# Sparse attention of a decoder trunk: probabilities times values in plain fp32 on two halves of TensorE's columns, in place of split fp32r products

## The chip, the core and the metric

The kernel runs on one core of one Trainium2 chip, as one launch. Its time is the device time of that core in microseconds (us). The program is built with a scheduling layer: the code says what each instruction does, and a scheduler decides within the dependences in which order the instructions of one engine stand. The engines run side by side, each through its own queue in order; semaphores that the layer inserts make one wait for another.

## The reference, cut to what matters

Two layers over 1024 tokens of width 1024, in float32. The second is native sparse attention: 16 heads of 64 in two groups that share keys and values. Every group of heads has three attentions over its keys, a compressed one (63 key blocks), a selected one (eight blocks of 64 keys) and a window of 512 keys, and their outputs are added with gates:

```python
o_cmp, p_cmp = compressed_attention(q, k_cmp, v_cmp, slopes)
o_slc = selected_attention(q, ks, vs, p_cmp, slopes)
o_win, _ = banded_attention(q, kw, vw, slopes, WIN_SIZE - 1, 1)
...
o = gates[..., 0:1] * o_cmp + gates[..., 1:2] * o_slc + gates[..., 2:3] * o_win
o = o.transpose(0, 3, 1, 2, 4).reshape(b, s, NSA_WIDTH).astype(x.dtype)
ym = memory_attention(qm, rms_norm(mem, mem_norm_g), w_mem_kv)
y = jnp.concatenate([o * jax.nn.silu(z), ym * jax.nn.silu(zm)], axis=-1)
return x + (y.astype(x.dtype) @ w_out)
```

The change is in the product of the probabilities with the values, for all three attentions, and in what prepares its two operands.

## The kernel before, in words

The first two thirds of the time are layer one and the projections of layer two (`proj`, L228, with `proj_step`, L238). Matmuls there and elsewhere are made from fp32r operands in split form: a value is rounded into a high part and the rest is a low part, and three products (high by high, high by low, low by high) stand for one of full precision.

`nsa_vals` (L1266) projects the values of both selected and window attention, 128 tokens at a time, and splits them: `vraw` is scaled by ScalarE, GpSimd rounds it into the first 64 columns of a `nv` tile (L1292, through L226) and puts the rest into the other 64 (L1293). So the weights of a later product hold 64 columns of high parts and 64 of low parts. `compress_v` (L1375) makes the same of the compressed values (`vc`).

`nsa_attention` (L1617) goes through 128 works. A work is one block of 128 queries of one group (`it`, 16 of them), one quad of heads, one branch (window or selected) and one pair of heads. A work has 1 to 8 blocks of 128 keys (`key_range`, L1483): 528 block-works in all. Its steps:

- `nsa_scores` (L1489): scores of two heads on TensorE (L1515); VectorE adds the mask and takes the minimum (L1524); ScalarE takes the exponential (L1526); VectorE the reciprocal of the sum (L1529); GpSimd scales by it and by the gate (L1532). Works are scored up to three ahead.
- `nsa_apply` (L1535): for two key blocks at a time TensorE transposes the probabilities of both heads into a PSUM bank `t` (L1545), ScalarE copies the bank to `ph` with rounding (L1549), VectorE subtracts `ph` from the bank into `pl` (L1550). The batch goes into a list `pend`, and the batch four places back (`DELAY = 3`) is multiplied.
- `nsa_av` (L1557): the product. For each key block one matmul with `ph` and one with `pl`, 256 columns (two heads) by weights of 128 columns, into an accumulator `acc`; the compressed part opens it (L1566). After the last key block of a quad ScalarE copies and VectorE adds the halves into `ot` (L1577, L1578), which joins high and low parts, and GpSimd multiplies it into the gate path `y` (L1581).

```python
        o = self.o[:, 256 * pair:256 * pair + 256]
        for x in (ph, pl):
            for i, k in enumerate(kbs):
                nc.tensor.matmul(o, V[:, k0 + k, :], x[:, 256 * i:256 * i + 256], start=False,
                                 stop=(br == 1 and k == nb - 1 and x is pl), skip_group_check=True)
```

Next to that, `nsa_cmp` (L1400) computes the compressed attention of a query block two ahead: its probabilities `ce` are transposed in eight pieces of 64 columns (L1449), copied and split into `pc` (L1450, L1451). As filler for TensorE, the loop runs projections of the second half of the tokens (`fill_proj`, L1781) and later the output projection of the first half (`out_half`, L1091, through `out_step` L1134). `out_tail` (L1141) is the output projection of the second half, which ends the program. The order in the code is the order of these calls; the scheduler moves instructions within what buffers (two or three `t` banks, two `acc` banks, nine `h` tiles for `ph`, `pl` and others) and data allow.

Of the kernel before, what the change touches and what calls it, by code (L numbers as in the profile page):

```python
# [38 lines left out]
BACK = 2  # L39
PAUSE = (1, 3, 5, 0)  # L40
LOOK = (3, 3, 2, 3)
DELAY = 3
FILL0, FILL1 = (4, 3, 2.2, 1.8), (3.2,)
CMPW = 2

# [1 line left out]
def f32(ap):  # L47
    return ap.bitcast(F32)


class Trunk:
# [1024 lines left out]
    def split_pair(self, half, p):  # L1076

        if (half, p) not in self.ys:
            for b in self.pend:
                h, g, _ = self.its[b[0][0]]  # L1080
                assert (h, 2 * g + b[0][1]) != (half, p)
            y = self.Y[half][p]
            self.Y[half][p] = None
            h = self.u("yh", F32R, (128, 2, 512))
            l = self.u("yl", F32R, (128, 2, 512))
            self.nc.scalar.activation(h, y, AF.Copy)  # L1086
            self.nc.vector.tensor_tensor(l, y, f32(h), op=ALU.subtract)
            self.ys[half, p] = (h, l)
        return self.ys[half, p]
# [176 lines left out]
    def nsa_vals(self, x, rcol):  # L1266
        nc = self.nc
        ws = []
        for i, kn in enumerate((3, 3, 2)):
            h, l = self.w()  # L1270
            ws += [(h[:, j, :], l[:, j, :]) for j in range(kn)]
        V = [[self.u("nv", F32R, (128, 8, 128)) for _ in range(2)] for _ in range(2)]
        self.gates = self.const.tile([128, 8, 48], F32, name="gates")
        half = self.small([128, 8], "half", bufs=1)
        nc.vector.tensor_scalar(half, rcol, 0.5, None, op0=ALU.mult)
        for tb in range(8):
            ps = self.big()
            for k in range(8):
                xh, xl = x[k][tb // 4]
                wh, wl = ws[k]  # L1280
                for i, (xx, w) in enumerate(((xh, wh), (xl, wh), (xh, wl))):
                    nc.tensor.matmul(ps[:, :304], xx[:, tb % 4 * 128:tb % 4 * 128 + 128], w,
                                     start=(k == 0 and i == 0), stop=(k == 7 and i == 2))
                if k % 4 == 3:
                    self.tick()
            nc.scalar.activation(self.gates[:, tb, :], ps[:, 256:304], AF.Tanh, scale=half[:, tb:tb + 1])
            v = self.h("vraw", F32, (128, 256))
            nc.scalar.activation(v, ps[:, :256], AF.Copy, scale=rcol[:, tb:tb + 1])
            for b in range(2):
                for g in range(2):  # L1290
                    o = 128 * b + 64 * g
                    self.round_to(V[b][g][:, tb, 0:64], v[:, o:o + 64])  # L1292
                    nc.gpsimd.tensor_tensor(V[b][g][:, tb, 64:128], v[:, o:o + 64],  # L1293
                                            f32(V[b][g][:, tb, 0:64]), op=ALU.subtract)
        self.V = V
        nc.vector.tensor_scalar(self.gates, self.gates, 0.5, 0.5, op0=ALU.mult, op1=ALU.add)

# [77 lines left out]
    def compress_v(self, ops):  # L1375
# [14 lines left out]
        for g in range(2):  # L1390
            p = self.bank()
            for c in range(2):
                nc.tensor.matmul(p[:, :64], h[:, c, g, :], w2[:, c, :], start=(c == 0), stop=(c == 1))
            v = self.const.tile([128, 128], F32R, name=self.n("vc"))
            nc.scalar.activation(v[:, 0:64], p[:, :64], AF.Copy)
            nc.vector.tensor_tensor(v[:, 64:128], p[:, :64], f32(v[:, 0:64]), op=ALU.subtract)
            out.append(v)
        self.vcmp = out

    def nsa_cmp(self, it):  # L1400
# [41 lines left out]
            nc.gpsimd.tensor_tensor(e, e, mx[:, 3, :, None].to_broadcast([128, 8, 64]), op=ALU.mult)  # L1442
        for _ in range(1 + CMPW):
            yield
        pcs = self.u("pc", F32R, (128, 2, 512))
        for quad in range(2):
            t = self.bank()
            for h in range(4):
                nc.tensor.transpose(t[:64, 128 * h:128 * h + 128], e[:, 4 * quad + h, :], self.ident)  # L1449
            nc.scalar.activation(pcs[0:64, quad], t[:64], AF.Copy)  # L1450
            nc.vector.tensor_tensor(pcs[64:128, quad], t[:64], f32(pcs[0:64, quad]), op=ALU.subtract)  # L1451
            yield
        self.pc[it] = pcs

    def nsa_query(self, it):
# [79 lines left out]
    def nsa_apply(self, W):  # L1535

        nc = self.nc
        nb = self.key_range(W)[1]
        for kb in range(0, nb, 2):
            kbs = list(range(kb, min(kb + 2, nb)))  # L1540
            w = 256 * len(kbs)
            t = self.bank()
            for i, k in enumerate(kbs):
                for h in range(2):
                    nc.tensor.transpose(t[:, 256 * i + 128 * h:256 * i + 128 * h + 128],  # L1545
                                        W["e"][h][:, 128 * k:128 * k + 128], self.ident)
            ph = self.h("ph", F32R)
            pl = self.h("pl", F32R)
            nc.scalar.activation(ph[:, :w], t[:, :w], AF.Copy)  # L1549
            nc.vector.tensor_tensor(pl[:, :w], t[:, :w], f32(ph[:, :w]), op=ALU.subtract)  # L1550
            self.pend.append((W["key"], kbs, nb, ph, pl))
            if len(self.pend) > DELAY:
                self.nsa_av(self.pend.pop(0))
            yield
        W["e"] = None

    def nsa_av(self, batch):  # L1557
        nc = self.nc
        key, kbs, nb, ph, pl = batch
        it, quad, br, pair = key  # L1560
        half, g, qb = self.its[it]
        k0 = self.key_range({"key": key})[0]
        V = self.V[1 - br][g]
        if br == 0 and pair == 0 and kbs[0] == 0:
            self.o = self.acc()
            nc.tensor.matmul(self.o, self.vcmp[g], self.pc[it][:, quad], start=True, stop=False,  # L1566
                             skip_group_check=True)
        o = self.o[:, 256 * pair:256 * pair + 256]
        for x in (ph, pl):
            for i, k in enumerate(kbs):  # L1570
                nc.tensor.matmul(o, V[:, k0 + k, :], x[:, 256 * i:256 * i + 256], start=False,  # L1571
                                 stop=(br == 1 and k == nb - 1 and x is pl), skip_group_check=True)
        if br == 1 and pair == 1 and kbs[-1] == nb - 1:
            av = self.o.rearrange("p (c e q) -> p c e q", c=2, e=2)
            tmp = self.h("ot", F32, (128, 2, 128))
            for e in range(2):
                nc.scalar.activation(tmp[64 * e:64 * e + 64], av[64 - 64 * e:128 - 64 * e, :, e, :], AF.Copy)  # L1577
                nc.vector.tensor_tensor(tmp[64 * e:64 * e + 64], av[64 * e:64 * e + 64, :, e, :],  # L1578
                                        tmp[64 * e:64 * e + 64], op=ALU.add)
            y = self.Y[half][2 * g + quad][:, :, qb % 4 * 128:qb % 4 * 128 + 128]  # L1580
            nc.gpsimd.tensor_tensor(y, y, tmp, op=ALU.mult)  # L1581

    def seg_load(self, seg):

# [32 lines left out]
    def nsa_attention(self, fill0, fill1):  # L1617
# [38 lines left out]
        for i, W in enumerate(works):  # L1656
# [27 lines left out]
            for sc in new:  # L1684
                run(sc)
            run(ap)
            if i % 8 == 7:
                self.AB.pop(it)
        while self.pend:
            self.nsa_av(self.pend.pop(0))  # L1690
        run(fill)

    def layer2_plan(self):
# [284 lines left out]
```

## Time and profile before

| what | us |
|---|---|
| median of 3 runs (1974.09 to 1976.76) | 1975.76 |
| the profiled execution, its own time | 1974.66 |
| its span, first to last instruction | 1972.9 |
| TensorE, busy share of the span | 96% |
| VectorE / ScalarE / GpSimd, busy share | 60% / 43% / 42% |
| attention stage, 1265 to 1905 us | 640 |

A profile's matmul row begins when the matmul starts to stream and ends when its last result has landed; matmuls overlap in the pipeline, so the mean duration of one is longer than the time from one start to the next. The latter, called pace here, is what a row of a dense sequence divided by its count gives. "PEld" is the loading of weights, which runs beside the matmuls. A line names the line of the kernel, the engine, the operation, and output <- inputs.

### The profile page before, as it was taken

The page shows a single profiled execution, that of the slowest core. Times are in us where ns is not written, and L with a number is a line of the kernel's source. Part 1 is how long each engine was busy: PE and PEld are TensorE (multiplying, and loading weights), DVE is VectorE, ACT ScalarE, POOL GpSimd, SP SyncE. Part 2 cuts the span into 40 slices and gives each one's busy share as a digit, 9 for nine tenths or more (in the row PEclk, how much of TensorE's full clock was granted, in tenths as well). Part 3 has the DMA queues.
Part 4 walks back from the last instruction along what each step waited for, and adds up shares of the span by engine and source line. Part 5 has one row for each costly group of instructions (what it writes and reads, how often), then busy time and mean ns, then how long its engine had stood idle before and what let it go on. Part 6 is the DMA issues. An engine that isn't in the chain of part 4 may idle for free. (4 is left out here: it accounts for less than half of the span.)

```text
span 1972.9 us, 27378 instructions
## 1 busy us (share of the span) xinstructions
PE 1885.7 (96%) x10018; PEld 1592.9 (81%) x10018; DVE 1187.7 (60%) x2293; ACT 840.0 (43%) x1780; POOL 824.7 (42%) x941
## 2 busy tenths in 40 slices
PE   8999999999999999999999999999988999989997
PEld 6789988887877777888888878787777787877886
DVE  7544336535344856561153574678688877889864
ACT  4210024423213623330044351467558666788851
POOL 6241102223124434322224433576676555567533
PEclk9999999999999999999999999999999999999998
DMA  4123310113110111132223413222231112210013
GB/s 177 61 97 122 114 53 33 33 54 107 54 51 25 43 43 43 42 131 81 78 74 93 138 60 112 75 75 70 65 94 57 49 49 80 89 57 33 12 58 99
DMA packets 57286, 141.90 MB, mean 72 GB/s; under 512 B 8256, under 2 KB 16960, under 8 KB 57152
## 3 DMA queue, kind: packets, MB, share of 16 engines
q1 hardware_dynamic: 57152, 140.16, 22.0%
q8 instruction: 79, 1.29, 0.3%
q14 instruction: 55, 0.45, 0.1%
HBM read 120.21 MB, written 19.92 MB: 71 GB/s over the span
## 5 line engine op out<-in xcount | busy, mean ns | idle before, releaser
L220 POOL TENSOR_SCALAR wh<-raw 128x1024 fp32r<-128x1024 f32 (+2 forms) x149 | 170.2, 1144 | 644.6 <-PE big L244 272.0
L221 DVE TENSOR_TENSOR wl<-raw,wh 128x1024 fp32r<-128x1024 f32 (+4 forms) x151 | 193.9, 1287 | 173.2 <-POOL wh L220 150.7
L1532 POOL TENSOR_SCALAR P<-P,nden,gates 128x640 f32<-128x640 f32 (+7 forms) x256 | 211.4, 835 | 136.3 <-DVE nden L1529 115.9
L244 PE MATMUL big<-xh,wh 128*128 128x512 f32 x752 | 259.0, 424 | 2.0 <-ACT xh L301 1.5
L244 PE MATMUL big<-xl,wh 128*128 128x512 f32 x752 | 243.4, 399 | 1.0 <-DVE xl L302 1.0
L244 PE MATMUL big<-xh,wl 128*128 128x512 f32 x752 | 234.4, 393 | 0.0
L1526 ACT ACTIVATE P<-P,nden 128x640 f32<-128x640 f32 (+7 forms) x256 | 187.6, 733 | 89.8 <-DVE nden L1524 84.4
L1550 DVE TENSOR_TENSOR pl<-t,ph 128x512 fp32r<-128x512 f32 (+1 forms) x304 | 183.7, 615 | 36.6 <-ACT ph L1549 32.6
L1549 ACT ACTIVATE ph<-t 128x512 fp32r<-128x512 f32 (+1 forms) x304 | 159.3, 533 | 58.9 <-PE t L1545 48.8
L1545 PE MATMUL t<-ident,P 128*128 128x128 f32 x1056 | 167.3, 277 | 16.5 <-DVE pl L1550 13.7
L244 PEld LDWEIGHTS big<-xl,wh 128*128 128x128 f32 x752 | 141.7, 189 | 32.4 <-DVE xl L302 2.6
L1545 PEld LDWEIGHTS t<-ident,P 128*128 128x128 f32 x1056 | 125.7, 141 | 50.5 <-DVE pl L1550 12.8
L244 PEld LDWEIGHTS big<-xh,wl 128*128 128x128 f32 x752 | 141.8, 189 | 30.1 <-DVE wl L221 0.2
L244 PEld LDWEIGHTS big<-xh,wh 128*128 128x128 f32 x752 | 135.3, 190 | 37.3 <-issue 14.9
L244 PE MATMUL big<-x,wh 128*128 128x512 f32 x480 | 144.3, 395 | 0.0
L1571 PE MATMUL acc<-ph,nv 128*128 128x256 f32 x528 | 129.1, 312 | 6.2 <-ACT ph L1549 5.9
L1571 PE MATMUL acc<-pl,nv 128*128 128x256 f32 x528 | 122.6, 300 | 0.0
L1524 DVE CUSTOM_DVE_ANT_0 P<-big,mask 128x640 f32<-128x640 f32 (+3 forms) x128 | 116.8, 914 | 3.6 <-PE big L1515 2.2
L244 PEld LDWEIGHTS big<-x,wh 128*128 128x128 f32 x480 | 87.8, 188 | 16.4
L1571 PEld LDWEIGHTS acc<-ph,nv 128*128 128x128 f32 x528 | 87.1, 192 | 13.8 <-ACT ph L1549 11.4
L524 DVE SCALAR_TENSOR_TENSOR df<-big,row 128x1024 f32<-128x1024 f32 x23 | 39.9, 1737 | 93.2 <-PE big L244 88.6
L244 PE MATMUL f<-x,wh 128*128 128x512 f32 x288 | 94.1, 405 | 0.0
(341 smaller groups left out, 4199.9 us busy)
## 6 DMA issues: line engine op xcount, KB each, us to landing
raw<-nw_f SPq DMA_DIRECT2D x42, 512.0 KB, 3.5
raw<-hw_dv SPq DMA_DIRECT2D x24, 512.0 KB, 3.5
raw<-hw_dil SPq DMA_DIRECT2D x22, 512.0 KB, 3.6
raw<-now SPq DMA_DIRECT2D x32, 256.0 KB, 2.7
raw<-hw_z SPq DMA_DIRECT2D x14, 512.0 KB, 3.4
raw<-how SPq DMA_DIRECT2D x16, 448.0 KB, 3.4
raw<-hw_xa SPq DMA_DIRECT2D x8, 512.0 KB, 3.5
res<-xT SPq DMA_DIRECT2D x8, 512.0 KB, 5.1
```

Source lines behind the costliest of these rows:

```text
L220: e.tensor_scalar(h[:, k0:k1], raw[:, k0:k1], 1.0, 0.0, op0=ALU.mult, op1=ALU.add)
L221: nc.vector.tensor_tensor(l[:, k0:k1], raw[:, k0:k1], f32(h[:, k0:k1]), op=ALU.subtract)
L244: self.nc.tensor.matmul(o, w[:, k, :], v, start=(k == 0 and i == 0), stop=(k == 7 and i == 2))
L524: self.nc.vector.scalar_tensor_tensor(ot[:, sl], p.rearrange("p (i r) -> p i r", r=dil), sc, rt[:, sl], op0=ALU.mult, op1=ALU.mult)
L1524: nc.vector.tensor_tensor_reduce(ev, sv, mv, scale=1.0, scalar=3e38, op0=ALU.add, op1=ALU.min, accum_out=den[:, 0, h:h + 1])
L1526: nc.scalar.activation(e, e, AF.Exp, bias=den[:, 0, h:h + 1], scale=-1.0, accum_out=den[:, 1, h:h + 1])
L1532: nc.gpsimd.tensor_scalar(es[h], es[h], den[:, 2, h:h + 1], gt[:, 2 - br, hh:hh + 1], op0=ALU.mult, op1=ALU.mult)
L1545: nc.tensor.transpose(t[:, 256 * i + 128 * h:256 * i + 128 * h + 128], W["e"][h][:, 128 * k:128 * k + 128], self.ident)
L1549: nc.scalar.activation(ph[:, :w], t[:, :w], AF.Copy)
L1550: nc.vector.tensor_tensor(pl[:, :w], t[:, :w], f32(ph[:, :w]), op=ALU.subtract)
L1571: nc.tensor.matmul(o, V[:, k0 + k, :], x[:, 256 * i:256 * i + 256], start=False, stop=(br == 1 and k == nb - 1 and x is pl), skip_group_ch ...
```

## The change

What is no longer made: the split of the values (`vraw`, L1292, L1293), of the compressed values, of the probabilities (`pl`) and of the compressed probabilities. `nv` becomes two plain fp32 tiles. The transposed probabilities are copied once, into `pt`: by VectorE for the second pair of key blocks of a work (`kb == 2`), by ScalarE for the others. The product is a plain fp32 matmul for each key block and each head: 64 columns of weights, 128 columns of moving data, head 0 into partitions 0 to 63 of the accumulator (the first half of TensorE's columns) and head 1 into partitions 64 to 127 (the second half). The compressed part has one block-diagonal weight tile for the two heads. VectorE multiplies the accumulator into `y` straight from PSUM. The products of a work are issued together, after the next work's transposes, once at least four key blocks are waiting (`BURST`, `nsa_due`); nothing ties them to each other beyond that.

```diff
-DELAY = 3
+BURST = 4
@@ nsa_vals
-            v = self.h("vraw", F32, (128, 256))
-            nc.scalar.activation(v, ps[:, :256], AF.Copy, scale=rcol[:, tb:tb + 1])
-            for b in range(2):
-                for g in range(2):
-                    o = 128 * b + 64 * g
-                    self.round_to(V[b][g][:, tb, 0:64], v[:, o:o + 64])
-                    nc.gpsimd.tensor_tensor(V[b][g][:, tb, 64:128], v[:, o:o + 64],
-                                            f32(V[b][g][:, tb, 0:64]), op=ALU.subtract)
+            nc.scalar.activation(V[tb // 4][:, tb % 4], ps[:, :256], AF.Copy, scale=rcol[:, tb:tb + 1])
@@ compress_v
+            v = self.const.tile([128, 128], F32, name=self.n("vc"))
+            nc.gpsimd.memset(v, 0.0)
+            for e in range(2):
+                nc.scalar.activation(v[64 * e:64 * e + 64, 64 * e:64 * e + 64], p[64 * e:64 * e + 64, :64], AF.Copy)
@@ nsa_cmp
+        t = self.bank()
+        for c in range(4):
+            nc.tensor.transpose(t[:, 128 * c:128 * c + 128], e[:, 2 * c:2 * c + 2, :].rearrange("p h n -> p (h n)"),
+                                self.ident)
+        pcs = self.u("pc", F32, (128, 512))
+        nc.scalar.activation(pcs, t, AF.Copy)
@@ nsa_apply
-            nc.scalar.activation(ph[:, :w], t[:, :w], AF.Copy)
-            nc.vector.tensor_tensor(pl[:, :w], t[:, :w], f32(ph[:, :w]), op=ALU.subtract)
-            self.pend.append((W["key"], kbs, nb, ph, pl))
-            if len(self.pend) > DELAY:
-                self.nsa_av(self.pend.pop(0))
+            pt = self.h("pt")
+            if kb == 2:
+                nc.vector.tensor_copy(pt[:, :w], t[:, :w])
+            else:
+                nc.scalar.activation(pt[:, :w], t[:, :w], AF.Copy)
+            W["p"] += [pt[:, 256 * i:256 * i + 256] for i in range(len(kbs))]
+            yield
+        W["e"] = None
+        self.pend.append(W)
+
+    def nsa_due(self, W=None):
+
+        due = [w for w in self.pend if w is not W]
+        if due and (W is None or sum(len(w["p"]) for w in due) >= BURST):
+            quad = due[0]["key"][:2]
+            while self.pend and self.pend[0] is not W and self.pend[0]["key"][:2] == quad:
                 self.nsa_av(self.pend.pop(0))
@@ nsa_av
+        c = 128 * (1 - br) + 64 * g
+        for k, pt in enumerate(W["p"]):
+            v = self.V[(k0 + k) // 4][:, (k0 + k) % 4, c:c + 64]
+            for h in range(2):
+                nc.tensor.matmul(self.o[64 * h:64 * h + 64, 128 * pair:128 * pair + 128], v,
+                                 pt[:, 128 * h:128 * h + 128], start=False,
+                                 stop=(br == 1 and k == nb - 1), skip_group_check=True)
-                nc.scalar.activation(tmp[64 * e:64 * e + 64], av[64 - 64 * e:128 - 64 * e, :, e, :], AF.Copy)
-                nc.vector.tensor_tensor(tmp[64 * e:64 * e + 64], av[64 * e:64 * e + 64, :, e, :],
-                                        tmp[64 * e:64 * e + 64], op=ALU.add)
-            nc.gpsimd.tensor_tensor(y, y, tmp, op=ALU.mult)
+            nc.vector.tensor_tensor(y, self.o.rearrange("p (c q) -> p c q", c=2), y, op=ALU.mult)
@@ nsa_attention
             run(ap)
+            self.nsa_due(W)
```

The order of the instructions moves with it. On TensorE, around the opening of one quad in the second half of the tokens, before (`L1566` opens the accumulator, `L1571` are the products, `L1545` transposes, `L1138` the filling output projection):

```order
L1566 MATMUL acc_13105<-pc_12279,vc_7895 128x512
L1571 MATMUL acc_13105<-ph_13023,nv_7302 128x256 x2
L1571 MATMUL acc_13105<-pl_13024,nv_7302 128x256 x2
L1138 MATMUL f_12937<-yh_12563,wp_13012 128x512
L1138 MATMUL f_12937<-yl_12564,wp_13012 128x512
L1138 MATMUL f_12937<-yh_12563,wp_13012 128x512
L1545 MATMUL t_13131<-ident,P_12926 128x128
L1545 MATMUL t_13131<-ident,P_12927 128x128
L1545 MATMUL t_13131<-ident,P_12926 128x128
L1545 MATMUL t_13131<-ident,P_12927 128x128
L1571 MATMUL acc_13105<-ph_13053,nv_7302 128x256 x2
L1571 MATMUL acc_13105<-pl_13054,nv_7302 128x256 x2
```

The same place now (`L1567` opens, `L1573` are the products, `L1539` the transposes, `L1508` scores); "x4" is two key blocks with two heads each:

```order
L1539 MATMUL t_12634<-ident,P_12447 128x128
L1539 MATMUL t_12634<-ident,P_12448 128x128
L1567 MATMUL acc_12643<-pc_11879,vc_7821 128x256
L1573 MATMUL acc_12643<-pt_12538,nv_7300 64x128 x4
L1573 MATMUL acc_12643<-pt_12562,nv_7300 64x128 x2
L1573 MATMUL acc_12643<-pt_12562,nv_7301 64x128 x2
L1573 MATMUL acc_12643<-pt_12567,nv_7301 64x128 x2
L1508 MATMUL big_12658<-KA_11387,A_11975 128x320 x2
L1508 MATMUL big_12658<-KB_11388,B_11976 128x320 x2
L1539 MATMUL t_12669<-ident,P_12513 128x128
L1539 MATMUL t_12669<-ident,P_12514 128x128
```

The products of a work stand in one run of ten where they stood in groups of two to four; over the whole program the 1056 products of `L1573` stand in 134 unbroken runs, 15 of them of a single product, most of 8 to 14.

On VectorE, at the end of the attention, before: one subtraction for each transposed bank, then the halves of the last quad.

```order
L1550 TENSOR_TENSOR pl_17039<-t_17033,ph_17038 128x512
L1550 TENSOR_TENSOR pl_17052<-t_17046,ph_17051 128x512
L1550 TENSOR_TENSOR pl_17065<-t_17059,ph_17064 128x512
L1550 TENSOR_TENSOR pl_17078<-t_17072,ph_17077 128x512
L1578 TENSOR_TENSOR ot_17097<-acc_16951,ot_17097 64x256 x2
```

Now: a copy for the second bank of each work, and the product with the gate path (`L1579`).

```order
L1543 COPY pt_16013<-t_16008 128x512
L1087 TENSOR_TENSOR yl_16033<-y_13879,yh_16032 128x1024
L1543 COPY pt_16048<-t_16043 128x512
L1543 COPY pt_16086<-t_16081 128x512
L1579 TENSOR_TENSOR y_13881<-acc_16020,y_13881 128x2x128
```

304 subtractions (`L1550`) and 64 additions (`L1578`) became 96 copies and 32 multiplications; the other banks are read by ScalarE alone.

## Rows read from the trace of the kernel before

**Rows 1.** Busy time of the engines by stage (x instructions), TensorE's granted clock, DMA.
```profile
0.00:1265.00 1265.00, 1242.44 (x5966) 1037.36 (x5967) 631.89 (x1003) 375.58 (x770) 397.83 (x460) 1.00 0.24 76
1265.00:1905.00 640.00, 587.75 (x3778) 509.16 (x3777) 524.82 (x1240) 448.75 (x983) 403.06 (x454) 0.99 0.18 59
1905.00:1972.90 67.90, 55.52 (x280) 46.40 (x278) 31.03 (x50) 15.72 (x27) 23.80 (x29) 0.92 0.37 113
```

**Rows 2.** Waits in 1265 to 1905 us: who waited for whom, total us, times, longest.
```profile
PE t L1545 <- DVE pl L1550: 13.7, 22, 1.6
PE s L1515 <- DVE nden L1524: 8.5, 11, 1.8
PE acc L1566 <- DVE ot L1578: 7.5, 7, 2.7
PE acc L1571 <- ACT ph L1549: 5.9, 13, 1.2
...
POOL P L1532 <- DVE nden L1529: 112.6, 55, 4.8
```

**Rows 3.** Groups by line and shape, TensorE: busy us, mean ns | idle before.
```profile
L1571 PE MATMUL acc<-ph,nv 128*128 128x256 f32 x528 | 129.1, 312 | 6.2 <-ACT ph L1549 5.9
L1571 PE MATMUL acc<-pl,nv 128*128 128x256 f32 x528 | 122.6, 300 | 0.0
L1408 PE MATMUL t<-kcbd,q 128*128 128x128 f32 x128 | 17.2, 278 | 0.2 <-DVE pl L1550 0.2
L1449 PE MATMUL t<-ident,ce 128*64 128x128 f32 x128 | 19.3, 274 | 7.7 <-POOL ce L1442 4.0 <-POOL ce L1439 1.8 <-DVE pc L1451 1.0
L1566 PE MATMUL acc<-pc,vc 128*128 128x512 f32 x32 | 14.5, 454 | 7.6 <-DVE ot L1578 7.5
```

**Rows 4.** Chain that ended last, in order of time: start us, us, what.
```profile
1717.57 0.47 PE acc L1571 x4
...
1719.45 0.89 PE t L1408 x8
...
1722.39 0.92 PE t L250 x8
```

**Rows 5.** One line's instructions: duration ns min/median/max.
```profile
L1408 PEld LDWEIGHTS t<-kcbd,q x128: 186/192/193, 1185.0 to 1812.2; 128*128 128x128 f32 x128
...
L1449 PEld LDWEIGHTS t<-ident,ce x128: 107/110/114, 1241.4 to 1830.4; 128*64 128x64 f32 x128
```

**Rows 6.** TensorE in order of time around a 64-column transpose: start us, us.
```profile
1278.37 0.28 PE L1571 MATMUL acc<-pl,nv 128*128 128x256 f32 x1
1278.49 0.60 PE L1449 MATMUL t<-ident,ce 128*64 128x128 f32 x4
1278.84 0.36 PE L1515 MATMUL s<-K,A 128*128 128x256 f32 x1
1279.05 0.28 PE L1515 MATMUL s<-K,B 128*128 128x256 f32 x1
1279.16 0.63 PE L244 MATMUL f<-x,wh 128*128 128x512 f32 x2
1279.64 0.39 PE L244 MATMUL f<-x,wl 128*128 128x512 f32 x1
```

**Rows 7.** Groups by line and shape, VectorE, ScalarE and GpSimd.
```profile
L1550 DVE TENSOR_TENSOR pl<-t,ph 128x512 fp32r<-128x512 f32 x224 | 152.2, 686 | 31.0 <-ACT ph L1549 27.9 <-POOL ssum L328 1.0 <-POOL y L1581 0.3
L1550 DVE TENSOR_TENSOR pl<-t,ph 128x256 fp32r<-128x256 f32 x80 | 33.4, 417 | 5.6 <-ACT ph L1549 4.7
L1578 DVE TENSOR_TENSOR ot<-acc,ot 64x256 f32<-64x256 f32 x64 | 26.7, 418 | 4.0 <-ACT ot L1577 3.1
L1451 DVE TENSOR_TENSOR pc<-t,pc 64x512 fp32r<-64x512 f32 x32 | 21.8, 684 | 6.2 <-ACT pc L1450 5.3
L1549 ACT ACTIVATE ph<-t 128x512 fp32r<-128x512 f32 x224 | 130.9, 590 | 50.4 <-PE t L1545 40.8 <-POOL y L1581 5.1 <-POOL wp L220 1.9
```

**Rows 8.** The split of the values, by tile: duration ns, first and last start us.
```profile
L226 POOL TENSOR_SCALAR nv<-vraw x32: 236/243/1215, 1063.1 to 1092.3; 128x64 fp32r<-128x64 f32 x32
```

## Prediction and its working

> **What bounds the kernel now.** I read the busy time by stage first, then the waits of the attention stage, then the groups of single operations, then dense stretches in order of time. The first view [rows 1] shows that only one of three stages matters here: the attention, 640 us long, in which TensorE is busy for 587.8, VectorE for 524.8 (82%), ScalarE for 448.8 (70%) and GpSimd for 403.1 (63%). The granted clock is 0.99 of full, so nothing is to be had from it. TensorE is the bound, and it stands still for 640 - 587.8 = 52.2 us. The second view [rows 2] shows whom it waits for: 13.7 us for the subtraction `pl`, which holds the transpose bank, 8.5 for VectorE to empty a score bank, 7.5 for `ot` to free the accumulator, 5.9 for the copy `ph`. So a change to this stage can pay in two ways: less TensorE time, or fewer of these waits.
>
> The projections before it and the tail behind it are touched little. The rounding and subtraction of the values on GpSimd (64 operations, the first kind of 0.24 us [rows 8]) end by 1093 us, 170 us before anything reads them. Their removal is costed at nothing: in the first stage TensorE is busy for 1242.4 of 1265 us [rows 1], and that is the cover.
>
> **The products, before.** Four products in a dense stretch of the chain take 0.47 us [rows 4], 0.1175 each; 528 with `ph` and 528 with `pl` [rows 3] are 1056 x 0.1175 = 124.1 us of TensorE.
>
> **The products, now.** The kernel before has a plain fp32 matmul of 128 columns: the scores of compressed attention. The code issues four of them for each of 16 query blocks, 64, and the trace has 128 records [rows 3]: a plain product is two records. Eight records in a row take 0.89 us [rows 4], 0.111 each. The changed kernel has 528 block-works x 2 heads = 1056 plain products of 128 columns, 2112 records. One after the other they take 2112 x 0.111 = 234.4 us. If the two halves of the columns work side by side, half: 117.2. No row shows two products side by side, so these are the two ends. In the order, products of the two halves alternate; with two records each, the second record of one half can run beside the first of the other, and the engine needs no reordering for it. I take the lower end: head 0 and head 1 share no columns, no output partitions and no data but the weights. Change: 117.2 - 124.1 = **-6.9 us**. Weights have to keep up. Eight records with two moving columns and 128 columns of weights take 0.92 us [rows 4], which is the loading alone, 0.115 each; beside 128-column streams it is hidden [rows 4, 5]. A load of 64 columns lasts 110 ns where one of 128 lasts 192 [rows 5]; at half of 0.115 the 2112 loads need 121 us, at the difference of the two durations, 0.082, they need 173. I take the first, since the two durations fall with the columns, so they fit under the streams almost exactly; the other end would add 56 us and stands in the range.
>
> The Trainium skill has a measured case for such packing (TensorE: Matmul & The Clock Gate, "Measured speedup vs the span model"): three column tiles gave 2.38 times, not 3. By that share two would give 1.59, an estimate of 147 us for the products, and the sum below would end near 1967 us.
>
> **The compressed part.** Opening the accumulator was 32 matmuls of 512 fp32r columns [rows 3]; two of that width take 0.48 us from start to start [rows 6], so 32 x 0.24 = 7.7. Now it is 64 records of 256 plain columns, twice 0.111 each: 14.2. **+6.5 us**. Its transposes fall from 128 [rows 3] to 64; four take about 0.43 [rows 6], so **-6.9**.
>
> **The waits.** VectorE loses the whole of `pl`, `ot` and the subtraction of `pc`: 152.2 + 33.4 + 26.7 + 21.8 = 234.1 us [rows 7]. It gains 96 copies, 80 of a full bank and 16 of half a bank. A copy is not in the trace; with the subtraction of the same size as the upper bound they cost 80 x 0.686 + 16 x 0.417 = 61.6 us; the other bound is a ScalarE copy's 590 ns less the fixed part that nothing here shows. I take the upper one, as it is the nearest row of the same engine [rows 7]. It gains 32 multiplications out of the accumulator, 0.418 each by the half-height addition [rows 7], 13.4. So its load falls from 524.8 to about 366 us, 57% of the stage. ScalarE gives away the 96 copies at up to 0.590 and falls to about 392. A transpose bank was held through ScalarE's 590 and then VectorE's 686 ns and the queue ahead of each; now through one copy. I let the wait for `pl` (13.7) and for `ot` (7.5) go, and two thirds of that for the score bank (5.7 of 8.5), since VectorE's queue is a third shorter: 26.9 us in 22 + 7 + 7 = 36 waits [rows 2]. An idle time counts from the landing of the last result; a matmul lasts 274 ns [rows 3] where its pace is 108, so each wait also uncovers 0.166 of pipeline: 6.0 more. **-32.9 us**. The wait for `ph` I leave: a product still needs its copy. Next in line is then `P` from GpSimd, whose own wait for VectorE's reciprocal, 112.6 us [rows 2], is the longest of the stage.
>
> **The end of the stage.** Before, the output projection stands between the last groups of products; in the new order the last 29 products follow each other and the projection comes behind all of them. Up to four microseconds of filler are missing where TensorE waits for the last probabilities; I take **+2**, between nothing and 4.
>
> **Sum.** -6.9 + 6.5 - 6.9 - 32.9 + 2 = -38.2 us. The profiled execution took 1974.66, 1.8 above its span and 1.1 below the median of 1975.76; 1974.7 - 38.2 = 1936.5. Forecast **1936 us**; its own range is 1912 to 1960: the lower end has nearly all of the 52.2 us of idle gone, the upper has half of the waits stay (16 us) and the weights slow the products by a few.
>
> **The rivals.**
> *Draining at every change of shape, chance 0.20.* The products stand in 134 runs between full-width work, so TensorE goes 268 times from full columns to halves or back. If its pipeline ran empty each time, that would be 268 x 0.166 = 44.5 us, and 1981; some of it falls where it would stand anyway, so 1950 to 1981. Against it: from the product at 1278.37 to the first 64-column transpose at 1278.49 is 0.12, the usual pace, and from there to the matmul at 1279.16 is 0.67, which is just four transposes at 0.108 and two matmuls at 0.118 [rows 6]. For it: those transposes use one half alone, and may not put the array into halves at all. The Trainium skill (TensorEngine Tiling (Array Packing), "Key Properties") says that changing the tiling mode, and not just the tile, drains TensorE; the rows around the narrow transposes do not show that.
> *The halves take turns, chance 0.25, the other side.* If a record on one half holds up the other, because moving data or weights come through one path, the products cost 234.4: 110.3 more than before. With the same waits gone: 1974.7 + 110.3 + 6.5 - 6.9 - 32.9 + 2 = 2054; TensorE would then hide what idle is left (52.2 - 32.9 = 19), so 2034 to 2054. That the change does not do what its text says, work on two halves at once, is this case. It decides from 0.0555 + 38.2 / 2112 = 0.074 us for each record: with less than two thirds of the overlap the kernel is slower. For it: nothing in the trace runs side by side. Against it: nothing in the operands makes them wait.
> *The waits stay, chance 0.05.* If transposes wait for `P` as long as they waited for the bank, only TensorE's own -7.3 + 2 is left: 1969.
>
> **How the numbers follow.** The forecast has 0.50. Faster or slower by over 0.2% (4 us, about what a measurement of this kernel can tell): the forecast's case is faster; of the draining case 0.09 is faster, 0.06 the same, 0.05 slower; the third is slower; of the last 0.03 faster, 0.02 the same. Faster 0.62, same 0.08, slower 0.30. The range 1908 to 2045 leaves out about 0.05 below and half of the case of turns, 0.13, above; cases of both signs lie in it, so the likeliest's own range stands above.
>
> **What would show it.** In the chain, eight records of `L1573` in a row: 0.45 us if side by side, 0.89 if by turns. At the start of a run: 0.17 us of nothing before its first product if it drains. In the waits, no line for `pl` and `ot`, and the new copy short. VectorE busy at about 57% of the attention stage, and the stage about 602 us long; the stage before it unchanged. The forecast is wrong if the stage grows while VectorE's share falls as said: then TensorE's products are the cause. If VectorE's share falls, the products take 117 us and the stage stays, the waits moved to `P`.

## The result, and the profile after

The changed kernel takes 1954.35 us, the median of 4 runs (1952.38 to 1956.07); the kernel before, on the same chip, 1975.81. The ratio is 0.9892 with an interval of 0.9875 to 0.9909: 1.1% faster, 21.5 us. The forecast of 1936 us was 18 us too low. The profiled execution took 1956.07 us, the slowest of the four; its span is 1954.3, 18.6 below the span before, and the difference of the two traces is told against that.

Busy time by stage, in the columns of [rows 1]:

```profile
0.00:1265.00 1265.00, 1242.44 (x5952) 1036.93 (x5953) 629.22 (x995) 375.10 (x770) 380.41 (x397) 0.99 0.24 76
1265.00:1885.00 620.00, 595.81 (x4804) 495.75 (x4803) 388.57 (x976) 369.77 (x811) 383.75 (x423) 1.00 0.19 61
1885.00:1954.30 69.30, 57.47 (x290) 48.61 (x288) 29.48 (x49) 14.97 (x25) 23.32 (x28) 0.93 0.36 111
```

The first stage is what it was. From its end to the last product is 639.8 us before (to 1904.8) and 619.4 now (to 1884.4); what is behind it grew from 68.1 to 69.9. VectorE fell from 524.8 to 388.6 us. TensorE's busy time did not fall, it rose from 587.8 to 595.8, though the products were to become cheaper.

Groups by line and shape in the attention stage, columns as in [rows 3] and [rows 7]:

```profile
L1573 PE MATMUL acc<-pt,nv 128*64 128x128 f32 x2112 | 150.9, 279 | 0.0
L1567 PE MATMUL acc<-pc,vc 128*128 128x256 f32 x64 | 19.3, 383 | 0.0
...
L1573 PEld LDWEIGHTS acc<-pt,nv 128*64 128x64 f32 x2112 | 118.4, 137 | 26.9 <-issue 26.2
...
L1543 DVE COPY pt<-t 128x512 f32<-128x512 f32 x80 | 54.8, 685 | 19.8 <-PE t L1539 19.6
L1579 DVE TENSOR_TENSOR y<-acc,y 128x256 f32<-128x256 f32 x32 | 13.4, 417 | 13.5 <-PE acc L1573 13.3
...
L1545 ACT ACTIVATE pt<-t 128x512 f32<-128x512 f32 x144 | 84.8, 590 | 69.8 <-PE t L1539 65.4 <-PE t L1458 3.3
```

Two rows matter. The products (first row) are 2112 records, two for each of 1056, as forecast, but TensorE is busy with them for 150.9 us, not 117. And the loading of their weights (third row) stood still for 26.2 us without anything that the profile could name as the reason ("issue"). In the chain of waits, here two runs of products (start us, us, what):

```profile
1602.39 1.24 PE acc L1573 x20
...
1653.21 1.68 PE acc L1573 x28
```

Eight records more take 0.44 us, 0.055 each: the two halves do work side by side, 2112 x 0.055 = 116 us. But twenty records take 1.24, not 1.10: 0.14 us belongs to the run and not to its records. TensorE in order of time around one run (start us, us, instruction):

```profile
1274.12 0.60 PE L1567 MATMUL acc<-pc,vc 128*128 128x256 f32 x2
1274.65 1.09 PE L1573 MATMUL acc<-pt,nv 128*64 128x128 f32 x16
1275.67 0.38 PE L1508 MATMUL s<-K,A 128*128 128x256 f32 x1
1275.90 0.28 PE L1508 MATMUL s<-K,B 128*128 128x256 f32 x1
```

The opening's two records need 2 x 0.222 = 0.44 [rows 4, eight of 128 columns in 0.89], the first product starts 0.53 after them: 0.09 too late. The sixteen records need 16 x 0.055 = 0.88, the score behind them starts 1.02 after the first: 0.14 too late. So this run costs about 0.23 us more than its records. The page cannot show this as idle time, since it draws an instruction to its modelled end; it shows it as "busy". The waits of the stage, TensorE's own first, then the largest (who for whom, total us, times, longest):

```profile
PE s L1508 <- DVE nden L1517: 5.2, 6, 1.8
PE t L1539 <- ACT pt L1545: 4.8, 4, 2.2
PE t L1539 <- DVE pt L1543: 4.0, 2, 2.8
...
ACT P L1519 <- DVE nden L1517: 122.8, 96, 5.1
POOL P L1525 <- DVE nden L1522: 111.6, 64, 4.8
...
PEld acc L1573 <- issue: 26.2, 128, 0.4
```

The last line counts the stops of the weight loads: 128 times, 0.2 us each on average, close to the number of runs (134). TensorE waits 6 times for a bank's copy (8.8 us) where it waited 22 times for `pl` and 13 for `ph` [rows 2], and for the accumulator not at all.

To close the sum I took the starts of all TensorE records of the stage. Each gets the usual distance to the next of its kind; what is over it stands at an edge of a run of products, or is a wait (over 0.12 us), or is small. The columns add up to the stage within 0.6. In us:

| kernel | usual pace | edges of runs (runs) | waits | small | stage | half clock |
|---|---|---|---|---|---|---|
| before | 542.4 | 0 (0) | 76.2 | 21.3 | 639.8 | 13.7 |
| after | 529.7 | 41.7 (134) | 29.1 | 18.8 | 619.4 | 3.4 |
| serial | 529.5 | 55.5 (133) | 15.4 | 64.9 | 665.2 | 0 |
| edge | 547.7 | 40.3 (139) | 26.6 | 12.2 | 627.4 | 10.2 |
| mid | 547.7 | 60.4 (225) | 17.4 | 22.5 | 648.5 | 6.8 |
| pin | 526.9 | 30.2 (99) | 57.0 | 15.4 | 630.0 | 23.9 |
| pinB | 527.8 | 29.5 (99) | 43.6 | 16.6 | 617.8 | 13.7 |
| burst6 | 526.9 | 34.7 (112) | 29.1 | 18.8 | 610.0 | 10.2 |
| burst8 | 526.9 | 32.9 (105) | 28.6 | 18.7 | 607.2 | 3.4 |
| nopl | 538.0 | 0 (0) | 65.6 | 18.0 | 621.6 | 27.3 |

The last column is time at the lower of the two granted clocks (1.2 GHz), in which records start at half their pace. It lies inside the others, and about half of it is lost, so some 5 us of what went from before to after are clock. Before to after: 13 us of TensorE's own work gone, 47 of waits gone, 42 come in at the edges of runs.

Not all of the 42 are changes of shape. From the record ahead of a run to the record behind it, the 82 runs with an even number of products cost 0.25 us more than their records (median), the 52 with an odd number 0.35: the product left over has no partner on the other half, and its two records take 0.22 in place of 0.11. That is about 38 us in all, 5 of them for products without a partner.

### The profile page after: what moved, and what is told of

It reads as the page before. It is cut to its first block, busy times and chain, and to the rows that moved or that the text cites. A ratio compares the mean times of both kernels' runs of the same rounds, so it can differ in the third digit from the quotient of the medians.

```text
span 1954.3 us, 28590 instructions
## 1 busy us (share of the span) xinstructions
PE 1895.7 (97%) x11042; PEld 1581.3 (81%) x11042; DVE 1047.3 (54%) x2019; ACT 759.8 (39%) x1606; POOL 787.5 (40%) x847
## 3 DMA queue, kind: packets, MB, share of 16 engines
q1 hardware_dynamic: 57152, 140.16, 22.6%
## 5 line engine op out<-in xcount | busy, mean ns | idle before, releaser
L1539 PE MATMUL t<-ident,P 128*128 128x128 f32 x1056 | 158.2, 275 | 9.0 <-ACT pt L1545 4.8
L1539 PEld LDWEIGHTS t<-ident,P 128*128 128x128 f32 x1056 | 127.4, 140 | 36.8 <-ACT pt L1545 6.9
L1573 PE MATMUL acc<-pt,nv 128*64 128x128 f32 x2112 | 150.9, 279 | 0.0
L1573 PEld LDWEIGHTS acc<-pt,nv 128*64 128x64 f32 x2112 | 118.4, 137 | 26.9 <-issue 26.2
L1545 ACT ACTIVATE pt<-t 128x512 f32<-128x512 f32 (+1 forms) x208 | 107.7, 522 | 75.8 <-PE t L1539 71.4
L244 PE MATMUL big<-x,wl 128*128 128x512 f32 x240 | 86.1, 391 | 1.2 <-DVE wl L221 1.2
L621 PE MATMUL big<-wh,xh 128*128 128x512 f32 x192 | 80.6, 420 | 0.5 <-DVE kbd L416 0.5
```

Source lines behind the costliest of these rows:

```text
L244: self.nc.tensor.matmul(o, w[:, k, :], v, start=(k == 0 and i == 0), stop=(k == 7 and i == 2))
L621: nc.tensor.matmul(ps, x, w[:, k, :], start=(q == k == j == 0), stop=(q == 3 and k == 1 and j == 2))
L1545: nc.scalar.activation(pt[:, :w], t[:, :w], AF.Copy)
L1573: nc.tensor.matmul(self.o[64 * h:64 * h + 64, 128 * pair:128 * pair + 128], v, pt[:, 128 * h:128 * h + 128], start=False, stop=(br == 1 an ...
```

## The experiments

My theory was: the products overlap fully; each run of them costs about 0.3 us for the two changes of shape, 42 us in 134 runs; the waits pay for more than that. Rivals: the products' own time, the hold on the transpose banks, the order.

**serial: do the halves really overlap?** All products of one head, then all of the other; a neighbour then mostly uses the same half.

```diff
-        for k, pt in enumerate(W["p"]):
-            v = self.V[(k0 + k) // 4][:, (k0 + k) % 4, c:c + 64]
-            for h in range(2):
+        for h in range(2):
+            for k, pt in enumerate(W["p"]):
+                v = self.V[(k0 + k) // 4][:, (k0 + k) % 4, c:c + 64]
```

> Edit: in the changed kernel the loop over the two heads goes outside the loop over the key blocks, so all products of one half of the columns stand before those of the other; same products, 133 runs in the order where the changed kernel has 134. Theory (the halves run side by side, two records started 6 ns apart every 109 ns): neighbours now sit on the same half, the 2112 records take about 0.109 each, 230 us in place of 115, and the kernel some 115 us more, 2050 to 2075 us. Rival (the pairs in the trace only look concurrent, the engine takes turns inside): no change beyond a few us, about 1955.

Measured in one run: 2001.69 us beside 1973.84 for the kernel before, 47 over the changed kernel. Twenty records in its chain of waits:

```profile
1794.61 1.95 PE acc L1573 x20
```

1.95 where the changed kernel takes 1.24. So it is two halves at work at once that make the products cheap. The price is half of what I expected, since the halves still overlap in part. In 132 of the 133 runs the starts fall into two rows, one for each half, with just as many records as the program has for it; within a row the records start 0.109 apart once it has begun. Where all products of one half stand before those of the other, the second row mostly begins while three records of the first are still to start, and as long as both rows go on, a record starts every 0.055. The trace does not name the half of a record, so this is a reading of the starts against the program. Waits fell as well (29 to 15 us) as TensorE got slower.

**edge and mid: what does a run cost?** A matmul of two columns over the full width is put in the products' way, into unread columns of the accumulator's bank: in `edge` ahead of the products of each work with more than two key blocks, where a change of shape mostly stands anyway, in `mid` between its second and third key block, where it breaks a run. Both issue 96 of them. (It opens the accumulator's bank anew, so what was summed there is lost; the work and its order are otherwise those of the changed kernel.)

```diff
@@ mid
         for k, pt in enumerate(W["p"]):
+            if k == 2:
+                nc.tensor.matmul(self.spare, self.ident, self.ones, start=True, stop=True, ...)
@@ edge
+        if len(W["p"]) > 2:
+            nc.tensor.matmul(self.spare, self.ident, self.ones, start=True, stop=True, ...)
         for k, pt in enumerate(W["p"]):
```

> Edit: the changed kernel with 96 extra full-width matmuls of two columns into unread columns of the accumulator's bank, each ahead of the products of a work with more than two key blocks, so beside full-width work; 139 runs in the order (134 without them). This is the control of the next kernel: it has the same extra matmuls. Both theories: 96 matmuls of two records at 0.111 are 21 us, and 5 runs more at 0.31 under two: about 1976 us; less where they fall into waits.

> Edit: the same 96 extra full-width matmuls, each between the second and the third key block of the work, so within the run of products; 225 runs in the order. Theory (a run costs 0.31 us by the accounts of four traces, 0.35 by its edges' starts, whatever its length): 86 runs more than its control, 27 to 30 us above it. Rival (what the edges show is the pipeline's normal filling, hidden in the sum): within 5 us of its control.

Measured: edge 1963.35 (ratio 0.9954, 0.9937 to 0.9971) with 139 runs, mid 1985.94 (1.0069, 1.0052 to 1.0087) with 225. The same instructions, 86 more runs, 22.6 us: 0.26 us a run. (`edge` itself came out some 13 us under the 1976 expected: by the table its extra matmuls are 18 us of TensorE's work and its stage is 8 us longer than the changed kernel's.) In `mid`, TensorE in order of time:

```profile
1324.45 0.60 PE L1568 MATMUL acc<-pc,vc 128*128 128x256 f32 x2
1324.98 0.66 PE L1576 MATMUL acc<-pt,nv 128*64 128x128 f32 x8
1325.57 0.38 PE L1573 MATMUL acc<-ones,ident 128*128 128x2 f32 x2
1325.88 0.88 PE L1576 MATMUL acc<-pt,nv 128*64 128x128 f32 x12
1326.68 0.38 PE L1573 MATMUL acc<-ones,ident 128*128 128x2 f32 x2
```

Eight records of products need 0.44 and the next matmul starts after 0.59; twelve need 0.66 and it starts after 0.80: 0.14 to 0.15 on the way out, whatever the length. Two records that are nothing but their loading take 0.23 [rows 4], the products behind start after 0.31: 0.08 on the way in. The theory's price stands, a little below what was expected. Part of it is given back: waits are 9 us shorter in `mid` than in `edge`.

**burst6 and burst8: fewer runs, the order left free.** Products are held back until six or eight key blocks are due.

```diff
-BURST = 4
+BURST = 6
```

> Edit: the changed kernel with bursts from six waiting key blocks on, the scheduler still free; 112 runs. Theory (0.31 us a run, and freedom keeps the waits as they are): 22 runs fewer, 7 us, about 1947. Rival (copies held longer cost as much as the runs save, as the two pinned kernels of 99 and 71 runs suggest, which differ by 2 us where 9 were expected): 1952 to 1958.

> Edit: the changed kernel with the scheduler free and bursts from eight waiting key blocks on; 105 runs, where bursts of six gave 112 and 1946.7 us. By 0.26 to 0.31 us a run 2 us less, 1945; rival: up to four more copies are held at once of nine buffers, and the transposes wait for them, 1950 or more.

Measured: burst6 1946.74 (0.9869, 0.9852 to 0.9885), burst8 1945.44 (0.9868, 0.9852 to 0.9884), both as expected, both faster than the kernel before, and equal to each other within their intervals. Against the changed kernel (0.9892, 0.9875 to 0.9909) the ratios are 0.2% lower, but the intervals still touch; in the profiled executions the stage is 9 and 12 us shorter. Runs fell from 134 to 112 and 105; the table has the edges 7 and 9 us lower and the waits where they were.

**pin and pin6: whole bursts by force.** Scheduling dependencies keep the products of a burst together, behind all TensorE work issued before and ahead of all issued after; `pin6` with `BURST = 6`.

```diff
+    def keep_bursts(self):
+        ...
+                if ins.name in self.burst:
+                    if prev is not None:
+                        self.tc.add_manual_dep(ins, prev, info, reason="burst")
+                    if self.burst[ins.name] != now:
+                        ...
+                        for s in since[-200:]:
+                            self.tc.add_manual_dep(ins, s, info, reason="burst")
+                    prev = ins.name
+                else:
+                    if prev is not None:
+                        self.tc.add_manual_dep(ins, prev, info, reason="burst")
+                    since.append(ins.name)
```

> Edit: every burst of products is kept together by ordering dependences on TensorE alone (its products follow each other, what was issued before stands before, what was issued after stands behind); 99 runs in place of 134, nothing else changed. Theory (each run costs about 0.35 us at its two edges, whatever its length): 35 runs fewer are worth 12 us, about 1942. Rival (the scheduler put the pieces where TensorE would have stood still, so the edges were free there): no gain or a loss, 1954 or more, with longer waits.

> Edit: as the pinned kernel, and a burst waits for six key blocks in place of four: 71 runs. Theory (0.35 us a run): 63 runs fewer than the changed kernel, 22 us, about 1932, if later release of the copies makes no new wait. Rival (copies held longer stall the transposes): the time lies above the pinned kernel's with waits for the copies' buffers in the trace.

Measured: pin 1967.86 (0.9972, 0.9959 to 0.9985) with 99 runs, pin6 1965.63 (0.9966, 0.9953 to 0.998) with 71. A miss: the edges fell by 11.5 and 20 us as the theory said, but the waits rose from 29.1 to 57.0 in `pin` and to about 60 in `pin6` (not in the table), and the rival, that the scheduler's freedom is worth more than the runs it adds, was right. Part of this rise is clock: `pin` has 23.9 us at the lower clock where the changed kernel has 3.4, so some 10 of the 28 us.

**pinB and pinB6: half of the pinning.** As `pin` and `pin6`, but work issued after a burst may move ahead of it.

```diff
                 else:
-                    if prev is not None:
-                        self.tc.add_manual_dep(ins, prev, info, reason="burst")
                     since.append(ins.name)
```

> Edit: of the pinned kernel's two kinds of ordering one alone: the products of a burst stand behind all that was issued before them on TensorE, while what is issued later (scores, filler) may move ahead of them; 99 runs, each burst whole. Question: which side of the pinning cost the 28 us of waits that the pinned kernel has more than the changed one. If it was later work that could no longer move ahead into a stall: the waits are those of the changed kernel and the shorter switching counts, 1940 to 1946. If it was the products themselves, ready but held behind transposes that still wait for their probabilities: as the pinned kernel, 1963 to 1970.

> Edit: the same one-sided ordering with bursts from six waiting key blocks on; 71 runs. By 0.31 us a run 9 us less than the kernel before it in this call; as the two-sided pair differed by 2 us alone, between 2 and 9 us less: 1931 to 1944 in the first case, 1957 to 1968 in the second.

Measured: pinB 1951.76 (0.9899, 0.9884 to 0.9914), between the two expectations; pinB6 1947.96 (0.988, 0.9863 to 0.9896), 4 us below it. The same 99 and 71 runs as with full pinning, 16 and 18 us less. So more than half of what pinning cost comes from the dependencies left out here, which keep later work from filling TensorE's waits; of the 12 us by which the two stages differ in the table, 5 are the lower clock (23.9 against 13.7 us at it). Even so the free order with 112 runs is level with the tied one with 71.

**holdpin and loadpin: is it the hold on the transpose banks?** On top of `pin`, VectorE does the subtraction of the kernel before again, into scratch: in `holdpin` it reads bank and copy and so holds the bank, in `loadpin` it reads the copy twice and the bank is free after the copy.

```diff
@@ holdpin
+            nc.vector.tensor_tensor(self.waste[:, :w], t[:, :w], pt[:, :w], op=ALU.subtract)
@@ loadpin
+            nc.vector.tensor_tensor(self.waste[:, :w], pt[:, :w], pt[:, :w], op=ALU.subtract)
```

> Edit: as the pinned kernel (99 runs), and VectorE again subtracts each copied bank from the transpose bank into a scratch tile that nobody reads, which holds the bank and loads VectorE as before; TensorE's work is that of the pinned kernel. Theory (the gain of the change comes from VectorE's relief, waits of 33 us by the prediction's sum, some 50 by the traces' difference): 35 to 55 us above the pinned kernel. Rival (the relief is worth little, the gain is TensorE's own): under 15 us above it.

> Edit: as the pinned kernel with the extra subtraction, but the subtraction reads the copy alone and not the transpose bank: VectorE is loaded as there, the bank is free after one copy. Theory (it was the bank held through two engines that made TensorE wait): most of the 80 us go, 1975 to 1995. Rival (it was VectorE's queue, behind which the mask and the reciprocal stand): most of the 80 us stay, 2020 to 2050.

Measured: holdpin 2048.1 (1.0382, 1.0356 to 1.0408), 80 over `pin` and well above the 35 to 55 expected; loadpin 2034.2 (1.0324, 1.0295 to 1.0353), 66 over it. In `holdpin` TensorE waits for the bank in plain sight (waits of its attention stage):

```profile
PE t L1562 <- DVE waste L1569: 45.8, 63, 2.5
```

In `loadpin` that line is gone and most of the loss stays, which would speak for VectorE's queue. But `loadpin` is no clean control, as the groups of VectorE and GpSimd show. Of `holdpin`:

```profile
L1569 DVE TENSOR_TENSOR waste<-t,pt 128x512 f32<-128x512 f32 x224 | 153.7, 686 | 27.1 <-ACT pt L1568 24.6
...
L1548 POOL TENSOR_SCALAR P<-P,nden,gates 128x640 f32<-128x640 f32 x80 | 72.0, 911 | 72.6 <-DVE nden L1545 59.4 <-DVE waste L1569 4.4 <-PE t L1562 3.6
```

and of `loadpin`:

```profile
L1569 DVE TENSOR_TENSOR waste<-pt 128x512 f32<-128x512 f32 x224 | 182.1, 813 | 17.0 <-ACT pt L1568 14.4
...
L1548 POOL TENSOR_SCALAR P<-P,nden,gates 128x640 f32<-128x640 f32 x80 | 89.9, 1133 | 50.9 <-DVE nden L1545 46.1 <-PE t L1562 2.9 <-PE big L1531 1.6
```

With both inputs in SBUF the subtraction lasts 813 ns in place of 686, 28 us more in 224, and GpSimd's scaling of `P` 1133 in place of 911. So it took the hold away and put another load in. What the pair shows is that 186 to 228 us more on VectorE cost 66 to 80 us in this kernel, although VectorE was idle for 244 us of the stage of `pin`; how much of it is the bank and how much the queue stays open. The lower clock is in it too: 41 us at it in `holdpin` and 65 in `loadpin`, beside the 24 of `pin`.

**nopl: the removed subtraction alone.** The kernel before, without `pl`; its products take `ph` twice, so the low parts are missing from the result and the high parts count double. (Two lines of `nsa_av` change with it, to tell the second pass from the first.)

```diff
-            pl = self.h("pl", F32R)
+            pl = ph
-            nc.vector.tensor_tensor(pl[:, :w], t[:, :w], f32(ph[:, :w]), op=ALU.subtract)
```

> Edit: the kernel before without the 304 subtractions; the product with the low parts is made with the high parts a second time, so TensorE does all the products it did, and the low parts of the probabilities are missing from the result. It is the forecast's third term by itself. Theory (VectorE's load was the source of TensorE's waits): the forecast had 13.7 + 5.7 us of waits and their pipeline, 24 us, for this; the accounts of the two traces have 47 us of waits gone in the changed kernel: 25 to 47 us less than before, 1925 to 1948. Rival (waits move to the probabilities from GpSimd, the changed kernel's gain is another): under 10 us less.

Measured: 1959.44 (0.9936, 0.9916 to 0.9955), 13 us less than before, between the two expectations. Its attention stage (columns as above) and TensorE's longest waits in it:

```profile
1265.00:1886.60 621.60, 575.48 (x3752) 509.63 (x3751) 368.65 (x938) 444.18 (x983) 401.10 (x450) 0.98 0.19 60
```

```profile
PE acc L1565 <- DVE ot L1577: 9.5, 7, 3.0
PE t L1545 <- ACT ph L1549: 8.2, 14, 1.8
PE s L1515 <- DVE nden L1524: 7.8, 8, 3.2
```

VectorE is busy for 368.7 us, less than in the changed kernel, and TensorE still waits: for `ot` as before, and for the bank now through ScalarE's copy. The table has its waits at 65.6, only 10.6 below the kernel before, and nearly 37 above the changed one. The lower clock hides some 7 us of the gain (27.3 us at it against 13.7). Even so VectorE's load alone does not explain the 47 us that went. I take the rest to come from what the other parts do together: the accumulator free after one multiplication, copies shared by two engines, products at a place of the scheduler's choosing, and a TensorE that is itself 42 us slower at the edges and so waits less. I did not take these apart, and no run here shows the share of each.

## Why the prediction was off

**The products, "117.2" side by side: right.** 0.055 a record, 116 us, and the loading hidden, by the lower end that was taken. The packing estimate of 1.59 from the Trainium skill did not apply: on one half records start 0.109 apart, on both together 0.055, a factor of 2.0. *The halves take turns* (chance 0.25) is out: its threshold was 0.074.

**Compressed part and end of the stage: right.** Opening at 0.22 a record as priced; behind the last product +1.8 against **+2**.

**VectorE.** The copy was priced at the subtraction's 686 ns and takes 685, the multiplication 417 against 418. Its load fell to 388.6 us (63%), not 366 (57%), although the list of what it loses and gains was complete: the durations of all its instructions in the stage, added one by one, fell from 593 to 437 us, by 156 where the forecast had 159. The busy time counts stretches in which two of its instructions overlap in the trace once, and there were 68 us of them before and 49 after, so taking a row's full duration out of the busy time takes out too much. ScalarE fell to 369.8, not 392: that its copies for `ot` and half of those for `pc` go too was left out.

**The waits, "-32.9": right in kind, too small.** TensorE's idle time in the profile fell from 52.2 to 24.2 us, 28.0 against a forecast of 26.9. But between starts the waits fell by 47, so 19 us more went with them where 6 were allowed; some 5 of these are the clock, of which the forecast said that nothing was to be had. And the reason given, VectorE's lighter load, carries only part of it (`nopl`).

**The step that failed is "Draining at every change of shape", which was made a rival with a chance of 0.20 and belonged in the sum.** Its price, 134 runs x 2 x 0.166 = 44.5 us, was somewhat high: the rows around runs give 0.23 a run, `mid` against `edge` 0.26, all starts added up 0.31, products without a partner included, which is 31 to 42 us. Its result, "1950 to 1981", holds the 1954. It was set aside because the 64-column transposes of [rows 6] cost nothing at either edge. Those rows were read rightly, but what they show of transposes does not carry over to products; the text had the doubt itself ("may not put the array into halves at all") without giving it weight. It is not that two halves have to be at work: the changed kernel has 15 runs of a single product, 13 of them on the half that the transposes used, and they pay as well. One of them (start us, us, instruction):

```profile
1519.93 0.82 PE L1539 MATMUL t<-ident,P 128*128 128x128 f32 x6
1520.68 0.43 PE L1573 MATMUL acc<-pt,nv 128*64 128x128 f32 x2
1521.04 0.50 PE L1138 MATMUL f<-yl,wp 128*128 128x512 f32 x1
```

Six transposes need 0.65, the product starts 0.75 after them; its two records need 0.22 on one half, the matmul behind starts after 0.36. Nor is it the number format: the opening of the accumulator is plain fp32 at full width, and the products behind it start 0.09 late all the same (at 1274 us above). Why the narrow transposes are free stays open. The rule that "changing tiling mode (not just tile) drains the TensorE" (the Trainium skill, TensorEngine Tiling (Array Packing), "Key Properties") agrees with the products, at 0.23 to 0.26 us a run; the narrow transposes show no drain.

**The sum again**, against the span: usual pace -12.7 (the forecast's -7.3; where the other 5 come from, filler that moved behind the stage or the sorting itself, is not shown), edges of runs +41.7, waits -47.1, small -2.5, end +1.8, together -18.8; the spans differ by 18.6. The forecast's -38.2 had the second term at nothing and the third at -32.9. That the time still lies within the likeliest case's own range (1912 to 1960) is in part luck, two errors against each other: 42 us of cost left out, about 14 of gain missed, and 5 more of TensorE's own.

## What to carry to other kernels

Packing two products into the two halves of the columns doubles their rate here, but each stretch of them pays about a quarter of a microsecond for going in and out, which the profile draws as busy: count stretches, not products, before using it, and make each long. Keep the pairs whole, since a product without a partner costs another 0.1 us. Make them long by asking for more work before one begins, and leave the scheduler free to fill; tying the order down removed 11 to 20 us of edges and brought about 30 us of waits, about a third of that through the lower clock. When a dummy operation stands in for a removed one, compare its own duration and its neighbours' first, since a change of one operand's memory can make it a different load.

## What the runs showed that I had not expected

- A narrow matmul is not in itself a change of shape: the transposes with 64 columns of weights cost nothing at their edges [rows 6], the products 0.23 us, even a single one on one half.
- The halves overlap even where the program does not alternate: in `serial` each half keeps its own pace of 0.109 us, and the second begins before the first has started its last three records.
- A VectorE subtraction with both inputs in SBUF took 813 ns in place of 686, and slowed GpSimd's operations beside it by a quarter (1133 against 911). The Trainium skill (GPSIMD Engine Reference, "Specifications") says that GpSimd shares its way to SBUF with VectorE and meets it on instructions with two SBUF inputs; these rows agree.
- Long waits cost clock as well. `loadpin`'s attention stage:

```profile
1265.00:1963.00 698.00, 615.87 (x4782) 506.66 (x4781) 579.73 (x1277) 374.69 (x811) 443.89 (x419) 0.95 0.17 54
```

  The granted clock is 0.95 of full (2.4 GHz) where the changed kernel has 1.00, and 65 us of it pass at the lower level (1.2 GHz), in 15 stretches; before each of them TensorE had stood waiting.
